# Other distances between the slots of one operand of the matmuls: x tiles 2,112 and 2,240 bytes apart in place of 2,048

## The chip, the cores and the metric

The kernel runs on one core of one Trainium2 chip. The metric is the device time of one execution in microseconds (us); of several executions the median is given. A matmul on TensorE (PE) takes two operands: a stationary one of up to 128 columns, which a weight load puts into the array beforehand (PEld), and a moving one, whose columns then stream through the array. Both are read from SBUF, a memory of 128 partitions in which a tile occupies the same bytes of every partition. The result goes to PSUM, from where VectorE (DVE) and ScalarE (ACT) fetch it. GpSimd (POOL) adds a few tiles, and SyncE (SP) issues the transfers from HBM.

## The reference

Four transformer blocks are computed one behind the other on 256 tokens of width 1,024, in float32. The first two have a feed-forward part and a gated projection behind the mixer:

```
for i in range(2):
    hn = rms_norm(h, norm_mix[i])
    h = h + (gla_mixer(hn, ...) if i == 0 else diff_attn_mixer(hn, ...))
    h = h + swiglu(rms_norm(h, norm_ffn[i]), ffn_w_in[i], ffn_w_out[i])      # inner width 2,816
    h = h + sigmoid(rms_norm(h, ple_norm[i]) @ ple_w_gate[i]) * (p[i] @ ple_w_proj[i])
h = h + short_conv_mixer(rms_norm(h, norm_g[0]), ...)    # four projections, a conv of width 3, one projection
h = h + moba_mixer(rms_norm(h, norm_g[1]), ...)          # four projections, 16 heads, one projection
```

Nearly all of the arithmetic is in the dense products of the normed activations with weight matrices.

## The kernel before

**Products.** Activations lie transposed, feature by token, in tiles of 128 partitions. Each float32 operand is split into a high part in float32r (a cast on ACT) and a low part (the rest, a subtraction on DVE), and a product is made of three matmuls, `mm3` (lines 211 to 213): high by high, then two mixed ones. The activation that a product reads is called x: `xh` and `xl`. A tile of x holds two k-blocks of 256 tokens, 2 x 256 x 4 = 2,048 bytes in a partition. `new_x` (line 118) takes such a pair of tiles from the pool `xp`, which has eight slots for each of the two names, handed out in turn. The eight `Norm`s take four pairs each, and so do the gated outputs of the mixers (`og`), the conv's y and the first eight of the 22 inner blocks of each feed-forward part (`S.spare` in `ffn_plan`). The other 14 inner blocks, `ah` and `al`, are tiles of 1,024 bytes in a pool of their own.

**Weights.** The weights come in units of up to 4 k-blocks x 256 columns, 4,096 bytes in a partition: `raw` by a transfer on SP's queue (4 slots), `whi` by an ACT cast at line 157 (6 slots), `wlo` by a DVE subtraction at line 166 (5 slots). `ahead` makes them some three units before they are used.

**Order.** `turn` runs one unit: 4 k-blocks x 2 halves x 3 matmuls, 24 in all, where a unit is full. In `gemm` the halves s = 0, 1 take the unit's two groups of 128 columns. Usually the weight is stationary and x moves, 256 columns; in the products called natural (q, k and v of the attention mixers, v of the first) x is stationary, 128 columns, and the weight moves, 256 columns. The rest of the work (norms, softmax, the attention's own matmuls) is put between the units by a table of due times, `DL`, counted in units. The table orders the instructions of each engine once, when the program is made; at run time they wait on semaphores alone.

**Where the tiles lie.** The pools stand one behind the other in a partition. As the program lays them out:

| tiles | first byte | distance | first byte modulo 512 |
|---|---|---|---|
| raw, 4 slots | 18,432 | 4,096 | 0 for all |
| whi, 6 slots | 34,816 | 4,096 | 0 for all |
| wlo, 5 slots | 59,392 | 4,096 | 0 for all |
| xh, 8 slots | 104,448 | 2,048 | 0 for all |
| xl, 8 slots | 120,832 | 2,048 | 0 for all |
| acc, sq, rb, t1, t2, px, small ones | 137,216 to 167,040 | | |
| ah, 14 tiles | 167,040 | 1,024 | 128 for all |
| al, 14 tiles | 181,376 | 1,024 | 128 for all |

Within a weight unit a stationary group of 128 columns is 512 bytes, so each begins at 0 modulo 512 too; the second half of an x tile begins 1,024 bytes behind the first. In the attention of the fourth block kh, kl, qh and ql lie at 128 modulo 512.

Of the kernel before, what the change touches and what calls it, by code (L numbers as in the profile page):

```python
# [13 lines left out]
F32R = mybir.dt.float32r  # L14
# [5 lines left out]
P = 128  # L20
D = 1024
KT = D // P
T = 256
# [66 lines left out]
def body(ctx: ExitStack, tc: tile.TileContext, a, out: bass.AP):  # L90
# [8 lines left out]
    xp = ctx.enter_context(tc.tile_pool(name="xp", bufs=8))  # L99
# [15 lines left out]
        return hp.tile([P, 2, T], F32, tag="h", name="h")  # L115

    def new_x():
        return [xp.tile([P, 2, T], F32R, tag=n, name=n) for n in ("xh", "xl")]

    def bank():  # L120
        return psg.tile([P, 2, T], F32, tag="g", name="g")
# [155 lines left out]
    class Norm:  # L277
# [6 lines left out]
        def part(self, i, h):  # L284
            p = self.gi
            xh, xl = new_x()
            gain = [sm("gain", p * 8 + 2 * i + j, 1) for j in range(2)]
            for j in range(2):
# [171 lines left out]
    def ffn_plan(layer):  # L460
# [4 lines left out]
        def done(ps, f):  # L465
            g, sg, t3 = t1(), t1(), t1()
            nc.vector.tensor_mul(g, ps[:, 0], N.rb)  # L467
            if f < 8:
                if f % 2 == 0:
                    S.spare = new_x()  # L470
                ah, al = S.spare[0][:, f % 2], S.spare[1][:, f % 2]
            else:
                ah, al = [S.fp.tile([P, T], F32R, tag=n, name=n, bufs=FT - 8) for n in ("ah", "al")]

            def lo():
                nc.vector.tensor_sub(al, t3, ah.bitcast(F32))
                S.act[f] = (ah, al)

            chain(layer, ("fs", lambda: nc.scalar.activation(sg, g, AF.Silu)),  # L479
                  ("fm", lambda: nc.vector.tensor_mul(t3, sg, ps[:, 1])),  # L480
                  ("fh", lambda: nc.scalar.copy(ah, t3)),
                  ("fl", lo))
# [13 lines left out]
    def gla_plan():  # L496
# [204 lines left out]
        def r_done(ps, h):  # L701
            b = SimpleNamespace()
            if h % 2 == 0:
                S.r4 = S.gp.tile([P, 2, 2, T], F32, tag="qk", name="rr", bufs=2)
            rr = S.r4[:, h % 2]
            nc.vector.tensor_mul(rr, ps, bc2(N.rb))

            def mul():
                b.o2 = t2()
                on("gr", h).tensor_mul(b.o2, S.on[h], rr)  # L710

            def hi():
                b.h, b.l = new_x()
                nc.scalar.copy(b.h, b.o2)

            def lo():
                nc.vector.tensor_sub(b.l, b.o2, b.h.bitcast(F32))
                S.og.update((2 * h + j, (b.h[:, j], b.l[:, j])) for j in range(2))

            chain(h, ("grs", lambda: nc.scalar.activation(rr, rr, AF.Silu)), ("grm", mul), ("grh", hi), ("grl", lo))  # L720
# [687 lines left out]
```

## Time and profile before

| | |
|---|---|
| time, median of 3 runs | 967.96 us (967.82 to 968.15) |
| the profiled execution | 970.79 us |
| its span, from the first to the last instruction | 969.0 us |
| PE busy, of its span | 947.2 us (98%) |
| DVE, ACT, POOL busy | 663.1, 556.8, 122.6 us |
| mean share of the full TensorE clock granted | 0.993 |

The busy time of PE is the union of the times in which some matmul is under way. Matmuls overlap in the array, so a single one lasts about 283 ns although the next begins long before that: the pace of a stream is the distance between the starts of two matmuls.

### The profile page before, as it was taken

The page shows a single profiled execution, that of the slowest core. Times are in us where ns is not written, and L with a number is a line of the kernel's source. Part 1 is how long each engine was busy: PE and PEld are TensorE (multiplying, and loading weights), DVE is VectorE, ACT ScalarE, POOL GpSimd, SP SyncE. Part 2 cuts the span into 40 slices and gives each one's busy share as a digit, 9 for nine tenths or more (in the row PEclk, how much of TensorE's full clock was granted, in tenths as well). Part 3 has the DMA queues.
Part 4 walks back from the last instruction along what each step waited for, and adds up shares of the span by engine and source line. Part 5 has one row for each costly group of instructions (what it writes and reads, how often), then busy time and mean ns, then how long its engine had stood idle before and what let it go on. Part 6 is the DMA issues. An engine that isn't in the chain of part 4 may idle for free.

```text
span 969.0 us, 19012 instructions
## 1 busy us (share of the span) xinstructions
PE 947.2 (98%) x7772; PEld 934.8 (96%) x7772; DVE 663.1 (68%) x988; ACT 556.8 (57%) x951; POOL 122.6 (13%) x86
## 2 busy tenths in 40 slices
PE   7899999999999989999999999999999999999998
PEld 6899999999999979999999999999999999999998
DVE  4893777656655698998586566565886667766653
ACT  5955666544544565676674454444774435677762
POOL 1060220000001462210010000012210003000010
PEclk9899999999999998999999999999999999999999
DMA  7543356555555734342565555565455537543332
GB/s 239 192 136 115 129 199 220 186 181 187 174 181 179 232 123 140 110 142 99 174 209 195 181 187 177 169 190 185 163 186 196 185 121 224 175 132 123 118 110 87
DMA packets 48007, 161.09 MB, mean 166 GB/s; under 512 B 5456, under 2 KB 6096, under 8 KB 47920
## 3 DMA queue, kind: packets, MB, share of 16 engines
q1 hardware_dynamic: 47376, 158.87, 50.1%
q10 hardware_dynamic: 544, 1.02, 0.4%
q8 instruction: 61, 1.00, 0.4%
q14 instruction: 26, 0.21, 0.1%
HBM read 158.81 MB, written 1.05 MB: 165 GB/s over the span
## 4 chain that ended last, share of the span: by engine, by line
PE 85%; DVE 8%; ACT 2%; DMA 2%; POOL 1%; issue 1%; SPq 0%; ACTq 0%; POOLq 0%; DVEq 0%
PE g L211 26%; PE g L212 26%; PE g L213 26%; DVE wlo L166 2%; DMA raw<-in_gla_i 2%; PE m L211 1%; ACT whi L157 1%; PE m L803 1%; PE m L981 1%; PE m L1181 1%; DVE t L446 1%; DMA raw<-in_moba_i 1%; PE m L638 1%; PE m L212 1%; DVE xl L293 1%
## 5 line engine op out<-in xcount | busy, mean ns | idle before, releaser
L211 PE MATMUL g<-xh,whi 128*128 128x256 f32 (+1 forms) x1672 | 478.3, 286 | 6.4 <-ACT whi L157 6.1
L213 PE MATMUL g<-xh,wlo 128*128 128x256 f32 (+1 forms) x1672 | 475.1, 284 | 0.4 <-DVE wlo L166 0.4
L212 PE MATMUL g<-xl,whi 128*128 128x256 f32 (+1 forms) x1672 | 474.9, 284 | 0.1
L166 DVE TENSOR_TENSOR wlo<-raw,whi 128x1024 fp32r<-128x1024 f32 (+2 forms) x315 | 378.2, 1206 | 95.0 <-PE g L213 51.7
L157 ACT CAST whi<-raw 128x1024 fp32r<-128x1024 f32 (+2 forms) x315 | 311.7, 995 | 135.1 <-PE g L212 105.1
L211 PEld LDWEIGHTS g<-xh,whi 128*128 128x128 f32 (+1 forms) x1672 | 322.3, 193 | 7.5 <-ACT whi L157 6.5
L213 PEld LDWEIGHTS g<-xh,wlo 128*128 128x128 f32 (+1 forms) x1672 | 322.1, 193 | 1.0 <-DVE wlo L166 1.0
L212 PEld LDWEIGHTS g<-xl,whi 128*128 128x128 f32 (+1 forms) x1672 | 322.4, 193 | 0.6 <-DVE xl L293 0.3
L211 PE MATMUL g<-whi,xh 128*128 128x256 f32 x448 | 131.2, 293 | 2.5 <-ACT xh L289 2.5
L213 PE MATMUL g<-whi,xl 128*128 128x256 f32 x448 | 127.9, 286 | 2.1 <-DVE xl L293 2.1
L212 PE MATMUL g<-wlo,xh 128*128 128x256 f32 x448 | 127.7, 285 | 0.0
L211 PEld LDWEIGHTS g<-whi,xh 128*128 128x128 f32 x448 | 86.9, 194 | 3.9 <-ACT xh L289 2.7
L213 PEld LDWEIGHTS g<-whi,xl 128*128 128x128 f32 x448 | 86.9, 194 | 2.3 <-DVE xl L293 2.3
L212 PEld LDWEIGHTS g<-wlo,xh 128*128 128x128 f32 x448 | 86.9, 194 | 0.0
L479 ACT ACTIVATE t<-t 128x256 f32<-128x256 f32 x44 | 18.4, 417 | 95.7 <-DVE t L467 95.7
L211 PE MATMUL g<-ah,whi 128*128 128x256 f32 x224 | 63.1, 282 | 0.0
L212 PE MATMUL g<-al,whi 128*128 128x256 f32 x224 | 63.0, 281 | 0.0
L213 PE MATMUL g<-ah,wlo 128*128 128x256 f32 x224 | 63.0, 281 | 0.0
L467 DVE TENSOR_TENSOR t<-g,rb 128x256 f32<-128x256 f32 x44 | 18.7, 424 | 62.8 <-PE g L213 62.1
L367 POOL TENSOR_TENSOR h<-h,pj 128x512 f32<-128x512 f32 x8 | 12.8, 1610 | 295.1 <-DVE h L383 288.8
L309 POOL TENSOR_TENSOR acc<-acc,sq 128x512 f32<-128x512 f32 x16 | 28.7, 1792 | 149.3 <-ACT sq L302 125.0
L289 ACT ACTIVATE xh<-h,small 128x256 fp32r<-128x256 f32 x64 | 29.3, 502 | 31.8 <-POOL h L451 9.3
(220 smaller groups left out, 1013.8 us busy)
## 6 DMA issues: line engine op xcount, KB each, us to landing
raw<-in_ffn_i SPq DMA_DIRECT2D x88, 512.0 KB, 4.0
raw<-in_ffn_o SPq DMA_DIRECT2D x40, 512.0 KB, 3.8
raw<-in_conv_i SPq DMA_DIRECT2D x32, 512.0 KB, 4.5
raw<-in_moba_i SPq DMA_DIRECT2D x32, 512.0 KB, 4.2
raw<-in_diff_i SPq DMA_DIRECT2D x24, 512.0 KB, 3.8
raw<-in_gla_i SPq DMA_DIRECT2D x23, 512.0 KB, 5.1
raw<-in_ple_g SPq DMA_DIRECT2D x16, 512.0 KB, 4.0
raw<-in_gla_o SPq DMA_DIRECT2D x5, 512.0 KB, 3.7
```

The source lines that it names most:

```text
L157: nc.scalar.copy(hi[:, :kn * c], raws[u][:, :kn * c])
L166: nc.vector.tensor_sub(lo[:, :kn * c], raws.pop(u)[:, :kn * c], hi[:, :kn * c].bitcast(F32))
L211: nc.tensor.matmul(ps, lh, rh, start=first, stop=False, **kw)
L212: nc.tensor.matmul(ps, lh, rl, start=False, stop=False, **kw)
L213: nc.tensor.matmul(ps, ll, rh, start=False, stop=last, **kw)
L289: nc.scalar.activation(xh[:, j], h[:, j], AF.Copy, scale=gain[j])
L293: nc.vector.scalar_tensor_tensor(xl[:, j], h[:, j], gain[j], xh[:, j].bitcast(F32), op0=ALU.mult, op1=ALU.subtract)
L309: on("sqa", p).tensor_add(self.acc, self.acc, q)
L367: nc.gpsimd.tensor_add(n, h, proj[p // 3][i])
L446: on(f"pm{i // 3}", layer).tensor_mul(m[:, j], t[:, j], proj[layer][i][:, j])
L467: nc.vector.tensor_mul(g, ps[:, 0], N.rb)
L479: chain(layer, ("fs", lambda: nc.scalar.activation(sg, g, AF.Silu)), ("fm", lambda: nc.vector.tensor_mul(t3, sg, ps[:, 1])), ("fh", lambda ...
```

## The change

`new_x` asks for tiles that are 16 (`xh`) or 48 (`xl`) elements longer than what is used, so that the slots lie (512 + 16) x 4 = 2,112 and (512 + 48) x 4 = 2,240 bytes apart. What the kernel gets is the first 512 elements of a slot in the old shape. Modulo 512 the eight slots of `xh` then begin at 0, 64, 128, 192, 256, 320, 384 and 448, and those of `xl` at 0, 192, 384, 64, 256, 448, 128 and 320. The slots of `xl` begin at 121,344, which is 0 modulo 512, and everything behind them moves by 2,048 bytes. No instruction is added or taken away.

```diff
     def new_x():
-        return [xp.tile([P, 2, T], F32R, tag=n, name=n) for n in ("xh", "xl")]
+        return [xp.tile([P, 2 * T + rest], F32R, tag=n, name=n)[:, :2 * T].rearrange("p (j c) -> p j c", c=T)
+                for n, rest in (("xh", 16), ("xl", 48))]
```

## Rows read from the trace of the kernel before

**Rows 1.** The page: busy time and instructions, granted clock, chain that ended last.

```profile
PE 947.2 (98%) x7772; PEld 934.8 (96%) x7772; DVE 663.1 (68%) x988; ACT 556.8 (57%) x951; POOL 122.6 (13%) x86
...
PE 85%; DVE 8%; ACT 2%; DMA 2%; POOL 1%; issue 1%; SPq 0%; ACTq 0%; POOLq 0%; DVEq 0%
PE g L211 26%; PE g L212 26%; PE g L213 26%; DVE wlo L166 2%; DMA raw<-in_gla_i 2%; PE m L211 1%; ACT whi L157 1%; PE m L803 1%; PE m L981 1%; PE m L1181 1%; DVE t L446 1%; DMA raw<-in_moba_i 1%; PE m L638 1%; PE m L212 1%; DVE xl L293 1%
```

**Rows 2.** Waits of PE: for whom, us in total, times, longest.

```profile
PE g L211 <- ACT whi L157: 6.1, 1, 6.1
PE m L529 <- DVE Z L520: 3.3, 1, 3.3
PE g L211 <- ACT xh L289: 2.5, 1, 2.5
```

**Rows 3.** Groups by line and shape, PE: count, busy us, mean ns, idle before.

```profile
L211 PE MATMUL g<-xh,whi 128*128 128x256 f32 x1664 | 475.1, 285 | 0.2
...
L211 PE MATMUL g<-whi,xh 128*128 128x256 f32 x448 | 131.2, 293 | 2.5 <-ACT xh L289 2.5
...
L211 PE MATMUL g<-ah,whi 128*128 128x256 f32 x224 | 63.1, 282 | 0.0
```

**Rows 4.** Timeline of PE, x moving, 250 to 260 us: start us, us.

```profile
250.10 0.28 PE L211 MATMUL g<-xh,whi 128*128 128x256 f32 x1
...
260.18 0.28 PE L211 MATMUL g<-xh,whi 128*128 128x256 f32 x1
```

**Rows 5.** Timeline of PE, ah and al moving, 286 to 296 us.

```profile
285.99 0.28 PE L211 MATMUL g<-ah,whi 128*128 128x256 f32 x1
...
295.96 0.28 PE L211 MATMUL g<-xh,whi 128*128 128x256 f32 x1
```

**Rows 6.** Weight loads by tile: duration ns lowest/median/highest, first and last start.

```profile
L211 PEld LDWEIGHTS g<-xh,whi x1672: 162/192/330, 6.1 to 964.1; 128*128 128x128 f32 x185, 128*96 128x96 f32 x1
...
L211 PEld LDWEIGHTS g<-ah,whi x224: 187/188/192, 270.1 to 676.7; 128*128 128x128 f32 x112
```

**Rows 7.** Timeline of PE behind two stops, x moving.

```profile
12.24 0.28 PE L211 MATMUL g<-xh,whi 128*128 128x256 f32 x1
12.37 0.28 PE L212 MATMUL g<-xl,whi 128*128 128x256 f32 x1
...
13.31 0.28 PE L211 MATMUL g<-xh,whi 128*128 128x256 f32 x1
...
13.91 0.28 PE L213 MATMUL g<-xh,wlo 128*128 128x256 f32 x1
...
710.85 0.28 PE L213 MATMUL g<-xh,wlo 128*128 128x256 f32 x1
...
711.91 0.28 PE L213 MATMUL g<-xh,wlo 128*128 128x256 f32 x1
```

**Rows 8.** Timeline of PE, x stationary and the weight moving, 373 to 375 us.

```profile
373.26 0.28 PE L211 MATMUL g<-whi,xh 128*128 128x256 f32 x1
...
374.94 0.28 PE L213 MATMUL g<-whi,xl 128*128 128x256 f32 x1
```

**Rows 9.** Timeline of PE, the same form behind a stop of 2.10 us.

```profile
363.31 0.58 PE L213 MATMUL g<-whi,xl 128*128 128x256 f32 x1 [2.10 <-DVE xl L293]
363.69 0.41 PE L211 MATMUL g<-whi,xh 128*128 128x256 f32 x1
...
368.60 0.37 PE L213 MATMUL g<-whi,xl 128*128 128x256 f32 x1
```

**Rows 10.** Stretches: busy us (x) of PE, PEld, DVE, ACT, POOL; granted clock, DMA share, GB/s.

```profile
363.80:368.50 4.70, 4.70 (x24) 4.70 (x24) 4.23 (x7) 2.33 (x2) 1.22 (x1) 0.50 0.69 229
500.00:680.00 180.00, 180.00 (x1506) 180.00 (x1506) 109.48 (x147) 87.25 (x121) 10.91 (x7) 1.00 0.58 187
```

**Rows 11.** Timeline of PE, scores of the fourth block, 128 columns moving.

```profile
845.77 0.27 PE L212 MATMUL m<-kl,qh 64*128 64x128 f32 x1
845.89 0.27 PE L213 MATMUL m<-kh,ql 64*128 64x128 f32 x1
846.00 0.33 PE L211 MATMUL m<-kh,qh 64*128 64x256 f32 x1
```

**Rows 12.** Writers of both kinds of tile: duration ns lowest/median/highest, first and last start.

```profile
L481 ACT CAST ah<-t x28: 404/405/406, 191.7 to 616.4; 128x256 fp32r<-128x256 f32 x28
...
L481 ACT CAST xh<-t x16: 399/406/407, 151.1 to 535.8; 128x256 fp32r<-128x256 f32 x16
...
L476 DVE TENSOR_TENSOR al<-t,ah x28: 424/425/425, 192.2 to 616.9; 128x256 fp32r<-128x256 f32 x28
...
L476 DVE TENSOR_TENSOR xl<-t,xh x16: 424/425/428, 151.5 to 536.2; 128x256 fp32r<-128x256 f32 x16
```

## The prediction

> **What bounds the kernel now.** I read the page first: PE is busy for 98% of the span, and the chain that ended last lies on PE for 85% of it, 26% on each of the three lines of `mm3` whose result is a bank of a product [rows 1]. The list of PE's waits is short: the three longest come to 11.9 us, each happens once, and all three belong to the beginning of a mixer, not to the long products [rows 2]. So the time is set by how fast PE gets through the matmuls of the products, and the question for a change of addresses is their pace. The groups by shape give their number [rows 3]: 3 x 1,664 in which x moves, 3 x 448 in which it is stationary, 6,336 with an operand from `xp`, and 3 x 224 that read `ah` and `al`.
>
> The mean duration in those groups doesn't show the pace, since matmuls overlap. The timeline does. With x moving, 84 matmuls start between 250.10 and 260.18 us: 10.08 / 84 = 120.0 ns each [rows 4]. With x stationary it is the same: 14 in 1.68 us, 120.0 ns [rows 8].
>
> [...]
>
> **Does the address play a part?** Two observations say so. First, `ah` and `al` go through the same line, with the same weights, shape and granted clock, as x in the very same chunk of `ffn_o`; they differ in where they lie: 128 modulo 512 against the weights' 0, where x has 0. Between 285.99 and 295.96 us 84 matmuls that read them start: 9.97 / 84 = 118.7 ns [rows 5]. Their weight loads are shorter too, 188 ns in the median against 192 for x [rows 6]. Second, behind a stop x itself is faster for a while: 9 matmuls in 1.07 us (118.9 ns) from 12.24 to 13.31 us and 9 in 1.06 us (117.8 ns) from 710.85 to 711.91 us, and then it settles: the five from 13.31 to 13.91 us are at 120.0 ns again [rows 7]. I read this as two readers, the stream and the load of the next stationary operand, that fall into one fixed step in which they meet every time. Equal places modulo 512 let that step hold; `ah` at another place never settles in it. That is an inference from two places, 0 and 128, and the trace has no third.
>
> The modulus can be narrowed. The two halves s of a chunk load weights that begin 512 bytes apart, and the pace is 120.0 ns through both, so what matters repeats at 512 or a divisor of it. And 128 differs from 0, so it is not 128 or less. With 512 the change gives eight places, with 256 four; in both cases not equal ones.
>
> **The change part by part.** It adds and removes no instruction, no wait and no transfer. It moves x, and all that lies behind x by 2,048 bytes, four times 512; so `ah`, `al` and the attention's tiles keep their places modulo 512, and I cost that at nothing. The engines that write x could notice the new starts. The cast and the subtraction that write `ah` and `al` at 128 take 405 and 425 ns in the median, those that write `xh` and `xl` at 0 take 406 and 425 [rows 12]. So that is nothing as well, and if it were some ns, 180 us of products leave DVE 70 us and ACT 93 us free [rows 10].
>
> What is left is the pace of the matmuls with x. How many set the end? The three lines hold 78% of the chain, 756 us of the 969.0 [rows 1]. `ah` and `al` are 672 x 118.7 ns = 80 us of this and the projections of p (`px`, 96 matmuls, not from `xp`) 12 us; 664 us remain, at 120.0 ns some 5,540 matmuls. The others of the 6,336 run where something else ends last, and speeding them up moves a wait.
>
> The new pace has bounds on both sides. [...] A nearer one is the scores of the fourth block: with only 128 columns moving, half the stream, two starts still take 0.23 us, 115 ns each, so the weight load by itself seems to hold about that [rows 11]; 5,540 x 5.0 ns = 28 us. From above: single distances of 0.13 us stand in the timeline (12.24 to 12.37 us) [rows 7], and an address at which each were like that would cost 5,540 x 10 ns = 55 us; but over nine starts no row shows more than 120.0 ns.
>
> I take 118.6 ns, between `ah` at 118.7 and the two stretches behind stops at 118.9 and 117.8 (118.4 together), nearer to `ah` since that is a steady state. With x in the new places the starts differ from slot to slot and, but for two slots in eight, between `xh` and `xl` of the same slot; a slot lasts 12 matmuls, hardly more than x takes to settle. So 5,540 x 1.4 ns = 7.8 us. About one in twenty of them already runs in the faster way behind a stop, which takes 0.4 us off: 7.4 us. The profiled execution, 970.79 us with a span of 969.0, would come to 963.4 with a span of 961.6. It lies 2.83 us above the median of the runs; from this median the forecast is 967.96 - 7.4 = 960.5 us.
>
> [...]
>
> **The rivals.**
> - *No change.* `ah` may be faster for another reason than its place modulo 512 (its tiles are 1,024 bytes, from a pool at other distances), or x may settle into the slow step at the new places too. Then the pace stays at 120.0 ns and the time at 967.96 us. For it: one place only is measured. Against it: `al` and `ah` are alike, and x is not bound to 120.0 either, as the stops show. A gain that goes into waits also ends here, but DVE and ACT have the room. Chance 0.12.
> - *Slower.* At some of the new places the readers settle into a step that is worse than 120.0 ns. The mechanism is the same, its place is lines 211 to 213, and it decides from a mean of 120.35 ns up (0.35 x 5,540 = 1.94 us, 0.2%). At 122 ns, a little less than the single 0.13 us distances and 2.0 above today, it would be 5,540 x 2.0 = 11 us, 979 us. For it: nothing says that the equal places are the worst. Against it: every departure from the step that the trace shows is a faster one on average. Chance 0.14.
> - *Much faster.* With eight places the meeting of the two readers is mostly avoided, down to what the load holds, 115 ns: 967.96 - 28 = 940 us; at 117 ns it is 951 us. [...] Against it: a stationary group of 512 bytes is read while 1,024 bytes of x stream, so the two pass over all places relative to each other, wherever they start. Chance 0.12.
> - That the change doesn't do what it says has no room: 2,112 and 2,240 are 64 and 192 more than a multiple of 512, which gives eight different starts.
>
> **How the numbers follow.** The forecast's case, a mean pace of 117.5 to 119.5 ns, has 0.62; its own range is 954 to 965 us (5,540 x 2.5 and x 0.5). A measurement of this kernel can tell about 0.2% from no change, 1.9 us. Faster: 0.62 + 0.12 = 0.74; within 0.2%: 0.12; slower: 0.14. For 8 in 10 I take the forecast's case, no change, and the shallower half of the much faster case: 947 us (a pace of 116.2 ns) to 970 us.
>
> **What would show it.** In the changed profile the timeline of the long products should have single distances that vary between 115 and 122 ns, at a mean near 118.6, where now each is 120.0; the weight loads of x should fall from 192 to about 188 ns in the median; `ah` should stay at 118.7. PE's waits should not grow by more than a microsecond or two. If the distances differ from slot to slot but are constant within one, each place has a step of its own; if the loads stay at 192 ns, x still settles and the prediction is wrong. [...]

## The result

The changed kernel takes 960.58 us in the median of four executions (959.03 to 962.59), the kernel before 968.06 us on the same chip (967.82 to 969.93). The ratio is 0.992 with a 95% interval of 0.9895 to 0.9945: faster by 0.8%, 7.5 us. Forecast were 960.5 us and 7.4 us. The profiled execution took 961.72 us, with a span of 959.9 where before it was 969.0 [rows 1]; this pair differs by 9.1 us, since the profiled execution of before, at 970.79 us, was a long one.

The page of the kernel after, to be held against [rows 1] (its lines 214 to 216 are 211 to 213 of before):

```profile
span 959.9 us, 19012 instructions
...
PE 935.1 (97%) x7772; PEld 922.8 (96%) x7772; DVE 664.0 (69%) x988; ACT 556.8 (58%) x951; POOL 118.8 (12%) x86
...
PE 80%; DVE 10%; DMA 3%; ACT 3%; issue 1%; POOL 1%; SPq 0%; ACTq 0%; DVEq 0%; POOLq 0%
PE g L216 24%; PE g L214 24%; PE g L215 24%; DVE wlo L169 4%; DMA raw<-in_gla_i 1%; DVE xl L296 1%; ACT whi L160 1%; PE m L214 1%; DVE t L449 1%; PE m L806 1%; PE m L984 1%; PE m L1184 1%; DMA raw<-in_ple_g 1%; PE m L641 1%; DMA raw<-in_moba_i 1%
```

The same instructions, DVE and ACT as busy as before; what has shrunk is PE's busy time, by 12.1 us, and the share of the three lines of `mm3` in the chain, from 78% to 72%. The stretch from 500 to 680 us, which had 1,506 matmuls under way before [rows 10], now has 1,521 (columns: busy us and instructions of PE, PEld, DVE, ACT, POOL; clock; DMA):

```profile
500.00:680.00 180.00, 180.00 (x1521) 179.95 (x1520) 111.07 (x146) 86.89 (x119) 11.48 (x7) 1.00 0.57 185
```

The timeline of PE inside it shows how. Where each distance was 120.0 ns [rows 4], they now vary, and 84 matmuls take 9.93 us, 118.2 ns each:

```profile
499.77 0.28 PE L216 MATMUL g<-xh,wlo 128*128 128x256 f32 x1
...
501.79 0.28 PE L215 MATMUL g<-xl,whi 128*128 128x256 f32 x1
501.90 0.28 PE L216 MATMUL g<-xh,wlo 128*128 128x256 f32 x1
502.02 0.28 PE L214 MATMUL g<-xh,whi 128*128 128x256 f32 x1
...
509.70 0.28 PE L216 MATMUL g<-xh,wlo 128*128 128x256 f32 x1
```

The weight loads of x have come down from 192 to 188 ns in the median, to where those of `ah` were and are [rows 6]:

```profile
L214 PEld LDWEIGHTS g<-xh,whi x1672: 186/188/330, 6.6 to 955.1; 128*128 128x128 f32 x185, 128*96 128x96 f32 x1
...
L214 PEld LDWEIGHTS g<-ah,whi x224: 187/188/189, 267.6 to 670.3; 128*128 128x128 f32 x112
```

Held against the program's own list of addresses, the single distances in this profile can be sorted by where the operand from `xp` begins (worked out from the starts of some 6,170 matmuls in steady work; mean ns, where x moves from the matmul's start to the next one, where x is stationary from the start before up to the matmul's own, while its load, some 0.19 us long, is under way):

| place modulo 512 | 0 | 64 | 128 | 192 | 256 | 320 | 384 | 448 |
|---|---|---|---|---|---|---|---|---|
| x moves | 119.1 | 119.9 | 118.8 | 116.3 | 118.8 | 118.5 | 119.1 | 117.4 |
| x stationary | 119.2 | 116.8 | 118.6 | 116.7 | 119.3 | 115.0 | 118.5 | 114.6 |

Together 118.2 ns. The places are not alike, and 192, 320 and 448 stand out. That is more than my theory says, by which any place but an equal one gives some 118.6 ns. So the experiments ask what the place does.

### The profile page after: what moved, and what is told of

Same layout as the page of the kernel before. It is cut to its first block, busy times and chain, and to the rows that moved or that the text cites. A ratio compares the mean times of both kernels' runs of the same rounds, so it can differ in the third digit from the quotient of the medians.

```text
span 959.9 us, 19012 instructions
## 1 busy us (share of the span) xinstructions
PE 935.1 (97%) x7772; PEld 922.8 (96%) x7772; DVE 664.0 (69%) x988; ACT 556.8 (58%) x951; POOL 118.8 (12%) x86
## 4 chain that ended last, share of the span: by engine, by line
PE 80%; DVE 10%; DMA 3%; ACT 3%; issue 1%; POOL 1%; SPq 0%; ACTq 0%; DVEq 0%; POOLq 0%
PE g L216 24%; PE g L214 24%; PE g L215 24%; DVE wlo L169 4%; DMA raw<-in_gla_i 1%; DVE xl L296 1%; ACT whi L160 1%; PE m L214 1%; DVE t L449 1%; PE m L806 1%; PE m L984 1%; PE m L1184 1%; DMA raw<-in_ple_g 1%; PE m L641 1%; DMA raw<-in_moba_i 1%
## 5 line engine op out<-in xcount | busy, mean ns | idle before, releaser
L214 PEld LDWEIGHTS g<-xh,whi 128*128 128x128 f32 (+1 forms) x1672 | 316.1, 189 | 7.9 <-ACT whi L160 6.6
L215 PEld LDWEIGHTS g<-xl,whi 128*128 128x128 f32 (+1 forms) x1672 | 316.7, 189 | 0.6 <-DVE xl L296 0.3
L216 PEld LDWEIGHTS g<-xh,wlo 128*128 128x128 f32 (+1 forms) x1672 | 316.2, 189 | 0.2 <-DVE wlo L169 0.2
```

Source lines behind the costliest of these rows:

```text
L214: nc.tensor.matmul(ps, lh, rh, start=first, stop=False, **kw)
L215: nc.tensor.matmul(ps, lh, rl, start=False, stop=False, **kw)
L216: nc.tensor.matmul(ps, ll, rh, start=False, stop=last, **kw)
```

## The experiments

Three theories. Theory 1 is the prediction's: equal places hold a slow step, any other place avoids it. Theory 2: each place has a pace of its own. Theory 3: what helps is that the place changes from matmul to matmul. Times are ratios to the kernel before on the same chip, with 95% intervals. In the shown timelines 84 matmuls start from the first row up to the last, unless another number is given.

**All slots of x at one place.** The slots keep their distance of 2,048 bytes; idle tiles ahead of and behind `xp`, N and 512 - N bytes, move all of x to N and leave the rest at its place modulo 512:

```diff
+    pre = ctx.enter_context(tc.tile_pool(name="pre", bufs=1))
     xp = ctx.enter_context(tc.tile_pool(name="xp", bufs=8))
+    post = ctx.enter_context(tc.tile_pool(name="post", bufs=1))
...
+    pad = pre.tile([P, N // 4], F32, name="pad", bufs=1)
+    nc.gpsimd.memset(pad[:, :1], 0.0)
+    pad2 = post.tile([P, (512 - N) // 4], F32, name="pad2", bufs=1)
+    nc.gpsimd.memset(pad2[:, :1], 0.0)
```

*Only the shift behind x* (no `pre`, 2,048 bytes in `post`):

> The slots of x stay 2,048 bytes apart and begin at 0 modulo 512 as before; only what lies behind x moves by 2,048 bytes, as it does in the change. One idle memset of one column is added. Theory 1 (equal places hold a slow step), theory 2 (each place has a pace of its own) and theory 3 (it is the alternation of places from matmul to matmul that breaks the step) all expect the pace of 120.0 ns and 968 us, within 0.2%. If the move of the other tiles were the cause, 960.6 us.

Measured: 1.0003 (0.9994 to 1.0012), and the pace in the long products is 120.0 ns. The move of the other tiles does nothing.

*N = 128:*

> All slots of xh and xl begin at 128 modulo 512, 2,048 bytes apart; the tiles behind keep their places modulo 512. Theory 1: x behaves as ah does, 118.7 ns, 5,540 x 1.3 = 7 us less, 961 us. Theory 2: the same, 118.8 ns where x moves, 961 us. Theory 3: no alternation, so 120.0 ns and 968 us.

Measured: 0.9952 (0.9933 to 0.9971), 963.63 us against 968.99. The pace is that of `ah`, 118.7 ns:

```profile
499.74 0.28 PE L215 MATMUL g<-xh,wlo 128*128 128x256 f32 x1
...
509.71 0.28 PE L215 MATMUL g<-xh,wlo 128*128 128x256 f32 x1
```

Theory 3 is out as the only cause: no place changes here. It also confirms that the place, not something else about `ah`, made it faster. Of the 7 us that the pace gives, 5 arrived. One product of this run, the last, is at 120.0 ns all the same, with x at 128:

```profile
940.04 0.28 PE L215 MATMUL g<-xh,wlo 128*128 128x256 f32 x1
...
950.12 0.28 PE L215 MATMUL g<-xh,wlo 128*128 128x256 f32 x1
```

*N = 192 and N = 448:*

> All slots of xh and xl begin at 192 modulo 512. Theory 1: any unequal place gives about 118.6 ns, so 960.5 us. Theory 2: the place has its own pace, which among the slots of the changed kernel was 116.3 ns where x moves and 116.7 where it is stationary: 4,400 x 3.7 + 1,140 x 3.3 ns = 20 us less, 948 us. Theory 3: 968 us.

> All slots of xh and xl begin at 448 modulo 512. Theory 1: 960.5 us. Theory 2: 117.4 ns where x moves, 114.6 where it is stationary: 4,400 x 2.6 + 1,140 x 5.4 ns = 17.6 us less, 950 us. Theory 3: 968 us.

Measured: 0.9843 (0.9810 to 0.9876) and 0.9838 (0.9811 to 0.9866), 953.89 and 951.58 us. Both are twice as good as the change, which theory 1 can't explain. But theory 2 as I had it, one pace for one place, is not the whole either. With all of x at 448 the profile shows two paces, each steady over long stretches, 117.7 and 113.3 ns:

```profile
499.83 0.28 PE L215 MATMUL g<-xh,wlo 128*128 128x256 f32 x1
...
509.72 0.28 PE L215 MATMUL g<-xh,wlo 128*128 128x256 f32 x1
...
714.73 0.28 PE L215 MATMUL g<-xh,wlo 128*128 128x256 f32 x1
...
724.25 0.28 PE L215 MATMUL g<-xh,wlo 128*128 128x256 f32 x1
```

*N = 256:*

> All slots of x begin at 256 modulo 512. Theory 2 (a pace of its own for each place, known from the slots of the changed kernel) with a pattern that repeats at 512: 118.8 ns where x moves, some 6 us less than before, ratio 0.993. With a pattern that repeats at 256, 256 is as equal to the weights' 0 as 0 is: 120.0 ns, ratio 1.000.

Measured: 1.0003 (0.9992 to 1.0014), and 120.0 ns in the long products:

```profile
499.81 0.28 PE L215 MATMUL g<-xh,wlo 128*128 128x256 f32 x1
...
509.89 0.28 PE L215 MATMUL g<-xh,wlo 128*128 128x256 f32 x1
```

In these runs the pattern repeats at 256 bytes. The "eight different places" of the change are four, and two slots of each name, at 0 and 256, are as equal to the weights as before. By this 192 and 448 are one place too, and their ratios, 0.9843 and 0.9838, agree. So do their paces: N = 192 also has 113.4 ns, 178 matmuls from 468.03 to 488.21 us. The two profiles part in one long stretch, where x at 448 takes 113.3 ns (above) and x at 192 takes 117.7:

```profile
714.74 0.28 PE L215 MATMUL g<-xh,wlo 128*128 128x256 f32 x1
...
724.63 0.28 PE L215 MATMUL g<-xh,wlo 128*128 128x256 f32 x1
```

With N = 192 this stretch holds 886 matmuls in a row, 700.13 to 804.48 us. At 4.4 ns each they are 3.9 us of the 5.2 between these two profiled executions (956.24 and 951.01 us). What differs there is the pace that a stretch has fallen into, not the place.

*N = 64 and N = 480:*

> All slots of x begin at 64 modulo 512. Theory 2, repeating at 512: 119.9 ns where x moves and 116.8 where it is stationary, as in the changed kernel's slots at 64: 4,400 x 0.1 + 1,140 x 3.2 ns = 4 us less, ratio 0.996. If the neighbours in time also count, the pace of a slot at 64 that follows others at 64 is not that of one among other places; then anything from 116 to 120 ns.

> All slots of x begin at 480 modulo 512, between 448 (116.2 ns when all lie there) and 0 (120.0 ns). If the pace changes gradually with the place: 118 ns, 11 us less, ratio 0.989. If x there stays in the step of 113 to 114 ns that a part of the matmuls at 448 has: 5,540 x 6.5 ns = 36 us less, ratio 0.963. If 32 bytes are too few to leave the equal step: 120.0 ns, ratio 1.000.

Measured: 0.9879 (0.9862 to 0.9897) and 0.9910 (0.9891 to 0.9929). At 64 the steady pace is 117.7 ns, not the 119.9 that slots at 64 had among others in the changed kernel: a slot's pace depends on its neighbours in time too. At 480 it is 118.3 ns. First x at 64, then at 480:

```profile
499.76 0.28 PE L215 MATMUL g<-xh,wlo 128*128 128x256 f32 x1
...
509.65 0.28 PE L215 MATMUL g<-xh,wlo 128*128 128x256 f32 x1
```

```profile
499.93 0.28 PE L215 MATMUL g<-xh,wlo 128*128 128x256 f32 x1
...
509.87 0.28 PE L215 MATMUL g<-xh,wlo 128*128 128x256 f32 x1
```

*N = 32 and N = 160:*

> All slots of x at 32 modulo 512. With all at 480, 32 below a multiple of 256, the pace was 118.3 ns. If the pace depends on how far x is from the weights in either direction: 118.3 ns, ratio 0.991. If the sign counts (x ahead of the weights or behind): anything from 113 to 120 ns.

> All slots of x at 160 modulo 512, between 128 (118.7 ns) and 192 (117.0 ns where x moves). Gradual change: 117.9 ns, ratio 0.988. If the step of 113.3 ns that some stretches at 192 and 448 have holds here: 5,540 x 6.7 = 37 us less, ratio 0.962.

Measured: 0.9860 (0.9845 to 0.9874) and 0.9962 (0.9947 to 0.9977). At 32 the pace is 116.7 ns; 32 above the weights is better than 32 below. At 160 there are again two: 120.0 ns from 499.80 us and 117.3 ns from 729.79 us, with slots that all lie alike. So it isn't gradual. First x at 32, then at 160:

```profile
499.73 0.28 PE L215 MATMUL g<-xh,wlo 128*128 128x256 f32 x1
...
509.53 0.28 PE L215 MATMUL g<-xh,wlo 128*128 128x256 f32 x1
```

```profile
499.80 0.28 PE L213 MATMUL g<-xh,whi 128*128 128x256 f32 x1
...
509.88 0.28 PE L213 MATMUL g<-xh,whi 128*128 128x256 f32 x1
...
729.79 0.28 PE L213 MATMUL g<-xh,whi 128*128 128x256 f32 x1
...
739.64 0.28 PE L213 MATMUL g<-xh,whi 128*128 128x256 f32 x1
```

**Relative or absolute.** 64 idle bytes ahead of the weights' slots move weights and x together:

```diff
+    pre = ctx.enter_context(tc.tile_pool(name="pre", bufs=1))
     wraw = ctx.enter_context(tc.tile_pool(name="wraw", bufs=RAWS))
...
+    pad = pre.tile([P, 16], F32, name="pad", bufs=1)
+    nc.gpsimd.memset(pad[:, :1], 0.0)
```

> 64 idle bytes ahead of the weights' slots: weights, x and everything behind them begin 64 bytes later, so x is at 64 as in the run with all of x at 64, but the weights are at 64 too. If what counts is where x lies relative to the weights: 120.0 ns for x, 118.7 for ah, ratio 1.000. If the place of x by itself counts: 117.8 ns and ratio 0.988.

Measured: 1.0012 (1.0002 to 1.0022), and x is back at 120.0 ns, though it lies at 64:

```profile
499.74 0.28 PE L214 MATMUL g<-xh,wlo 128*128 128x256 f32 x1
...
509.82 0.28 PE L214 MATMUL g<-xh,wlo 128*128 128x256 f32 x1
```

So what counts in these runs is where x lies relative to the weights: with x alone at 64 the pace was 117.7 ns. That the other tile is the matmul's second operand, and not one of the many others from which x moved away, can be seen where x is stationary and the weight moves: the two places change sides. With x at 32 that pace is 118.2 ns, within 0.1 of what x moving had at 480; with x at 480 it is 116.6, within 0.1 of what x moving had at 32 (71 matmuls each of the same product, x at 32 first):

```profile
802.86 0.28 PE L213 MATMUL g<-whi,xh 128*128 128x256 f32 x1
...
811.25 0.28 PE L215 MATMUL g<-whi,xl 128*128 128x256 f32 x1
```

```profile
807.12 0.28 PE L213 MATMUL g<-whi,xh 128*128 128x256 f32 x1
...
815.40 0.28 PE L215 MATMUL g<-whi,xl 128*128 128x256 f32 x1
```

So in these runs the pace goes by the start of the moving operand less that of the stationary one, modulo 256.

**Half of the change.**

```diff
+        return [xp.tile([P, 2 * T + rest], F32R, tag=n, name=n)[:, :2 * T].rearrange("p (j c) -> p j c", c=T)
+                for n, rest in (("xh", 16), ("xl", 0))]
```

> One half of the change: the slots of xh 2,112 bytes apart, those of xl 2,048 as before and at 0 modulo 512. Two of the three matmuls of each product read xh. By the mean over places in the changed kernel, 118.5 ns, and 120.0 for the third with xl: 5,540 x 1.0 ns = 5.5 us less, ratio 0.994. If the equal step comes back with every matmul that reads xl: ratio 1.000.

Measured: 0.9945 (0.9929 to 0.9960), 5.2 us of 968.58, as expected from the means; xl at the equal place does not bring the slow step back for all. A surprise stands in its profile: `ah` and `al`, at 128 as ever, run at 120.0 ns (71 matmuls in 8.52 us), where before they had 118.7 [rows 5]. So the second pace is not peculiar to x; and the place alone does not set it, since `ah` lies at 128 modulo 512 here as before.

```profile
283.24 0.28 PE L213 MATMUL g<-al,whi 128*128 128x256 f32 x1
...
291.76 0.28 PE L212 MATMUL g<-xh,whi 128*128 128x256 f32 x1
```

**The change without its poor places.** Slots 2,176 bytes apart, the first at 64 by idle tiles of 64 and 448 bytes as above (left out here), so that they lie at 64 and 192 modulo 256 in turn:

```diff
+        return [xp.tile([P, 2 * T + 32], F32R, tag=n, name=n)[:, :2 * T].rearrange("p (j c) -> p j c", c=T)
+                for n in ("xh", "xl")]
```

> The change with its four useful starts alone: slots of xh and xl 2,176 bytes apart from a first one at 64, so that they begin at 64, 192, 320, 448 modulo 512, which is 64 and 192 modulo 256; neither 0 nor 128. If a slot's pace is that of its place: 117.8 ns or a little less, 5,540 x 2.2 = 12 us less, ratio 0.987 or below. If a change of place from slot to slot is what frees the readers, no better than the change: ratio 0.992.

Measured: 0.9838 (0.9821 to 0.9854), 952.91 us. In the long products 84 matmuls take 9.75 us, 116.1 ns:

```profile
499.82 0.28 PE L216 MATMUL g<-xh,wlo 128*128 128x256 f32 x1
...
509.57 0.28 PE L216 MATMUL g<-xh,wlo 128*128 128x256 f32 x1
```

With N = 192 and N = 448 this is the best of all, and faster than both the kernel before and the change. In this stretch all of x at 64 and all of x at 192 take 117.7 ns each, so a mixture can be faster than either of its places alone, which neither expectation said. I did not try to combine them, nor other places for `ah`.

## Why the prediction was right, and what in it was not

- **The bound.** PE's pace sets the time: shown. The pace of the products changed and the time followed; DVE and ACT had the room, 663.1 and 556.8 us busy before, 664.0 and 556.8 after.
- **The address plays a part.** Shown by N = 128, 192 and 448 against the shift alone. That it is the place relative to the weights, as I took for granted, is shown by the joint shift of 64 bytes (120.0 ns, against 117.7 with x alone at 64) and by the paces that change sides when x is stationary.
- **The modulus.** I left 256 and 512 open. In these runs it is 256: N = 256 is the kernel before again, at 120.0 ns and 1.0003. The change's eight places are four, and one of them, with a quarter of the slots, is the equal one; even by 512 slot 0 of each name was equal. "In both cases not equal ones" was wrong, and the price, one value for all 5,540 matmuls, left it out.
- **The pace of 118.6 ns.** It measured 118.2 ns (118.5 where x moves, 117.1 where it is stationary); `ah` stayed at 118.6, as forecast. The reason I gave for it, that every unequal place leaves the slow step for about the same faster way, fell: the places run from 113.3 to 120.0 ns. `ah` was a fair stand-in only because the change mixes poor places and good ones. So my size was nearly right as the mean of a mixture that I did not see: that is luck.
- **The count.** Over all steady matmuls with x, some 6,200, the mean distance fell from 119.9 to 118.2 ns: 1.7 ns, which is 10.5 us, and 9.4 us on the 5,540 of the chain, 2 us more than I priced. Some of it went into waits, as forecast in kind, with 3 us a little more than "a microsecond or two": the ten largest entries of PE's waits come to 17.2 us before and 20.2 after. That 7.4 us were forecast and 7.5 measured is two errors that cancel, the gain in pace taken too small and the waits left out: luck as well. The 9.1 us between the two spans hold another 2 us that are not the pace: some 52 matmuls of before ran at a granted clock of 0.50 and some 30 of after. At that clock [rows 10] 23 starts take 4.91 us [rows 9], 213.5 ns each, 93 more than 120.0; 22 x 93 ns are the 2 us. The largest waits after, to be held against [rows 2]:

```profile
PE g L214 <- ACT whi L160: 6.6, 1, 6.6
PE g L214 <- ACT xh L292: 3.0, 2, 2.7
PE m L614 <- POOL t L608: 2.2, 1, 2.2
PE m L532 <- DVE Z L523: 2.1, 1, 2.1
```

- **The rivals.** No change would have needed the slow step at the new places too; over a whole run that holds for 256 alone, at a ratio of 1.0003. "Slower" fell: no place has a pace above 120.0 ns for long, and the kernel that is nearest to slower, the joint shift, is at 1.0012. Its price leaned on "single distances of 0.13 us", which are an effect of rounding to 0.01 us: in the trace's own nanoseconds that distance is 121. "Much faster" was the rival that I undervalued: with x at 448 the kernel reaches 951.58 us and for long stretches 113.3 ns. Its lower bound of 115 ns, read from [rows 11], was rounded too: the two distances there are 113 ns each, so the best stretch stands just at that bound; that the load sets it is not shown. My argument against it, that the two readers pass over all places anyway, is refuted by that stretch.
- **The loads as a sign.** They fell from 192 to 188 ns as forecast, but they don't tell the pace: `ah` had its 118.7 ns with loads of 188 [rows 5, 6], and over all of the run at 448, with its paces of 117.7 and 113.3 ns, the median of one line is 188 and that of another 192, as before the change.

```profile
L213 PEld LDWEIGHTS g<-xh,whi x1672: 162/192/329, 6.3 to 944.4; 128*128 128x128 f32 x185, 128*96 128x96 f32 x1
L215 PEld LDWEIGHTS g<-xh,wlo x1672: 161/188/329, 6.9 to 944.6; 128*128 128x128 f32 x185, 128*96 128x96 f32 x1
```

**What stays open.** Why one place can hold two paces (128: 118.7 and 120.0 ns; 160: 120.0 and 117.3; 192 and 448: 117.7 and 113.3), and what sends a stretch into the one or the other. It seems to differ between executions of one program too: four of the kernel with N = 192 spread from 949.72 to 956.24 us, where before 13 lay within 967.12 to 970.39. That the cause is two reads of SBUF that meet is an inference from the relative place; no run here looks into the memory itself.

## What to carry to other kernels

When PE is the bound, read the pace from the starts of its matmuls, not from their durations, and compare it with the same form of matmul elsewhere in the trace: another pace for equal work is a lead. Where moving and stationary operand begin at the same place modulo 256 bytes, try a few other distances between them; other distances between the slots were worth 0.8% with poor places among them, and good places 1.6%, here. All of this is float32r with 256 columns moving and a weight load before each matmul; other forms were not tried. Don't count on one pace for one place: measure the kernel, since the same place held two paces here.

## What the runs showed of the hardware

| x begins behind the weights by, modulo 512 | steady pace, x moving | ratio |
|---|---|---|
| 0 (kernel before), 256, 0 with both at 64 | 120.0 ns | 1, 1.0003, 1.0012 |
| 32 | 116.7 ns | 0.9860 |
| 64 | 117.7 ns | 0.9879 |
| 128 | 118.7 ns, 120.0 in the last product | 0.9952 |
| 160 | 120.0 or 117.3 ns | 0.9962 |
| 192 | 117.7 or 113.4 ns | 0.9843 |
| 448 (192 modulo 256) | 117.7 or 113.3 ns | 0.9838 |
| 480 (224 modulo 256) | 118.3 ns | 0.9910 |

That the relative place of two operands in SBUF changes the pace of float32r matmuls by up to 5.6% (113.3 against 120.0 ns), at a mean granted clock of 0.995 in the run with x at 448 and 0.993 in the profiled execution of before, I had not expected.
